# A four-layer network in one kernel: scalar work moved into the feed-forward loops, low-rank transposes between two chunks, two heads normalised on ACT

## The chip, the core and the metric

The kernel runs on one core of one Trainium2 chip. The metric is the device time of one execution, in microseconds; the number given is the median of several executions. TensorE (PE in the profile) multiplies matrices, VectorE (DVE), ScalarE (ACT) and GpSimd (POOL) work elementwise, SyncE (SP) issues the weight transfers. Each engine takes its own instructions strictly in order, and waits on semaphores for the others.

## The reference, cut to what matters

One sequence of 256 tokens with 1024 features goes through four layers in fp32. `first_block` has two: pooling and causal attention, then a gated linear recurrence (RG-LRU), each followed by a gated feed-forward network (FFN) with a three-tap causal convolution and 2816 hidden features. `second_block` has two hybrid layers:

```python
h = rms_norm_2(x, g_mix);  proj = h @ w_in          # c_q c_kv k_r d_q d_k d_v s_q s_k s_v gates
q = (rms_norm_2(c_q, g_q_lora) @ w_uq)              # low rank: 256 -> 8 heads of 96
kv = (rms_norm_2(c_kv, g_kv_lora) @ w_ukv)          # low rank: 128 -> 8 heads of 64 + 64
o_mla = softmax(rope(q) @ rope(k).T) @ v            # 8 heads
o_diff = (softmax_1 - lam * softmax_2) @ d_v        # 4 heads, position bias
o_win = window_attention(s_q, s_k, s_v, sink)       # 8 heads, position bias, band of 128
x = x + (sum of sigmoid(gate_b) * (o_b @ w_branch_b)) @ w_out
x = x + (gelu(conv(h @ w_gate)) * (h @ w_up)) @ w_down
x = x + sigmoid(rms_norm_2(x, g_ple_in) @ w_ple_gate) * rms_norm_2(pe @ w_ple_proj, g_ple)
```

The recurrence needs `softplus(-rg_lambda)`; `lam` is made of two exponentials of dot products; `rope` needs the cosine and sine of positions times 16 frequencies; the position biases need |q - k| as a 256 by 256 table.

## The kernel before, in words

All activations stay on the chip, 256 tokens as two halves (t) of 128. The weights (252 MB) are streamed once: `_push` (L247) issues the transfer of the next chunk of 128 x 2048 on SP, and ACT and DVE split it into a high part `hi` (L262) and a residual `lo` (L263), in two halves of 1024 columns each. `chunk` (L269) keeps two chunks ahead of the one in use; a buffer is free for the next chunk when TensorE has finished with the chunk three before. Each product is three matmuls (`mm3`, L277: high x high and the two mixed ones), 128 x 512 or 128 x 256 at a time. PSUM has eight banks under four tags: A (3), S (2), T (2), O (1).

The stages follow each other in `build` (L334): pooled attention, FFN, recurrence, FFN, hybrid layer 0, hybrid layer 1, each hybrid layer ending with an FFN and a gated addition of `pe`. The order of the instructions on each engine is made by a scheduler from the program order, which serves as priority, and from its own estimate of when operands are ready: an instruction may rise past earlier ones that are not ready. What goes through `vec_o`, `act_o`, `pool_o` or `sync_o` (`InOrder`, L199) is pinned behind the instruction written just before it for the same engine; in the attention of a hybrid layer TensorE too is pinned (L1272).

What the change touches:

- `norm` (L368) opens a stage: the residual sum is updated on DVE (L339), eight feature tiles are transposed (L384) and split into `xh` (ACT, L389) and `xl` (DVE, L390), and the first matmuls follow. `norm_rows` (L404) makes the row factors.
- `ffn` (L608): 22 rounds j. Each takes one chunk of two 128-wide columns blocks (48 matmuls), scales, convolves, gates (L638, L649) and splits the result; every second round from j = 5 on also multiplies a chunk of the down projection (24 matmuls of 512 columns).
- `softplus` (L656) computes two small factors for the recurrence: 2 instructions on ACT (absolute value, exponential) and, with the two halved biases of L695, 28 on DVE, all pinned. `rglru` (L688) calls it ahead of its `norm`.
- `before_b` (L795) runs between the start of the second FFN and its loop (L614): `positions` (L747) loads positions and band on POOL's queue, makes the distance tables and the cosine and sine (24 DVE instructions, 3 on ACT), then `layer_scalars(0)` (L799; 18 on DVE, 2 exponentials on ACT). `layer_scalars(1)` runs at the head of hybrid layer 1 (L1203). All are pinned.
- `hybrid` (L1199): `mla_prep` (L926) makes the low-rank vectors c, `proj` (L1021) the difference queries dq and keys dk, two chunks each; then `mla_low_rank` (L949) transposes c (6 transposes, L956) and splits it (L958, L959), and `mla_heads` (L963) multiplies by the next weights.
- `heads` (L1060) writes out the attention as bursts by hand: each burst names some steps (queries and keys `mq`, scores and softmax `ms`, transposes `mt`, values `mo` of two heads) and how many pieces of the query, gate and branch projections follow on TensorE. `normal` (L1071) multiplies the exponentials of a head by the reciprocals of their sums on POOL (L1074); `normalise` (L922) does the same on ACT.
- Behind the attention, ahead of the FFN, `pe` is loaded on POOL's queue (L1291) and split (L1293; the split's own lines are L311 and L312), not pinned.

Of the kernel before, what the change touches and what calls it, by code (L numbers as in the profile page):

```python
# [19 lines left out]
P = 128  # L20
S = 256
# [188 lines left out]
class Net:  # L210
# [69 lines left out]
        mm(out, ah, bl, start=False, stop=False)  # L280
        mm(out, al, bh, start=False, stop=stop)  # L281

    def tm_block(self, banks, n, xh, xl, nk, per):

        for k0 in range(0, nk, per):
            wh, wl = self.chunk(per, n)
            for t in range(2):
                for k in range(per):
                    kk = k0 + k
                    self.mm3(banks[t][:, :n], xh[:, kk, t * P:t * P + P], xl[:, kk, t * P:t * P + P],  # L290
                             wh[:, k, :], wl[:, k, :], kk == 0, kk == nk - 1)
# [178 lines left out]
    def pool_attn(self):  # L470
# [64 lines left out]
            self.split(ah[:, c, :], al[:, c, :], ob[:, :S])  # L535

        u = proj("AA")
        mt = self.t([P, 4, 384], "w6")
        self.sync_o.dma_start(mt, self.ap["pool"].rearrange("p (g c) -> p g c", g=4))
        pw = self.t([P, 4, P], "hg")  # L540
# [64 lines left out]
                                    in1=self.rb[:, None, :].to_broadcast([P, 2, S]), op=ALU.mult)  # L605
        return z

    def ffn(self, gi, body, ahead=None):  # L608
        xh, xl = self.norm(gi, self.acc)
        first = self.fm_first(xh, xl)  # L610
        self.norm_rows()
        acc = None
        if ahead is not None:
            ahead()  # L614
        done = []
        for j in range(NF):
            if j % 2 == 0:
                hh, hl = self.t([P, 2, S], "hg", F32R), self.t([P, 2, S], "hg", F32R)
                done.append((hh, hl))
            z = self.times_r(self.t([P, 2, S], "s"), first[j] if j < 2 else self.fm(xh, xl, "TS"[j % 2]))  # L620
            m = body(j, z[:, 0, :], z[:, 1, :])
            self.split(hh[:, j % 2, :], hl[:, j % 2, :], m)
            if j % 2 and j > 2 * LAG:
                if acc is None:
                    acc = self.wide_banks()
                kk = j - 1 - 2 * LAG
                self.tm_wide(acc, *done[kk // 2], kk, False)
        for kk in range(NF - 2 * LAG, NF, 2):
            self.tm_wide(acc, *done[kk // 2], kk, kk == NF - 2)
        self.acc = acc  # L630

    def ffn_a(self, l, gi, ahead=None):
        nc = self.nc

        def body(j, u, g):
            u = self.conv(u, f"fw{l}", f"fb{l}", j, 3, (2, 1, 0))
            g = self.conv(g, f"fw{l}", f"fb{l}", NF + j, 3, (2, 1, 0))
            nc.scalar.activation(g, g, AF.Gelu_apprx_tanh)  # L638
            nc.vector.tensor_tensor(out=g, in0=g, in1=u, op=ALU.mult)
            return g  # L640

        self.ffn(gi, body, ahead)

    def ffn_b(self, i, gi):
        nc = self.nc

        def body(j, u, g):
            g = self.conv(g, f"cw{i}", f"cb{i}", j, 3, (1, 0, -1))
            nc.scalar.activation(g, g, AF.Gelu_apprx_tanh)  # L649
            nc.vector.tensor_tensor(out=g, in0=g, in1=u, op=ALU.mult)  # L650
            return g

        self.ffn(gi, body)


    def softplus(self):  # L656

        nc = self.nc
        v = self.vec_o
        lam = self.vecs[:, self.vat["rlam"]:self.vat["rlam"] + NR]  # L660
        tl = lambda: self.t([P, 16], "ty")[:, :NR]
        e, den, s, s2, acc, out, half = (tl() for _ in range(7))
        self.act_o.activation(e, lam, AF.Abs)
        self.act_o.activation(e, e, AF.Exp, scale=-1.0)
        v.tensor_scalar(den, e, 2.0, None, op0=ALU.add)
        v.reciprocal(den, den)
        v.tensor_tensor(out=s, in0=e, in1=den, op=ALU.mult)
        v.tensor_tensor(out=s2, in0=s, in1=s, op=ALU.mult)
        v.tensor_scalar(acc, s2, 1.0 / 19, 1.0 / 17, op0=ALU.mult, op1=ALU.add)
        for n in (15, 13, 11, 9, 7, 5, 3, 1):  # L670
            v.tensor_tensor(out=acc, in0=acc, in1=s2, op=ALU.mult)
            v.tensor_scalar(acc, acc, 1.0 / n, None, op0=ALU.add)
        v.scalar_tensor_tensor(acc, acc, 2.0, s, op0=ALU.mult, op1=ALU.mult)
        v.tensor_scalar(out, lam, -1.0, 0.0, op0=ALU.mult, op1=ALU.max)
        v.tensor_tensor(out=out, in0=out, in1=acc, op=ALU.add)
        r4 = self.t([P, NR], "rg4")
        r2 = self.t([P, NR], "rg2")
        v.tensor_scalar(r4, out, -4.0, None, op0=ALU.mult)
        v.tensor_scalar(r2, out, 2.0, None, op0=ALU.mult)
        return r4, r2  # L680

    def after(self, ins, group):

# [4 lines left out]
    def rglru(self, gi):  # L688
        nc = self.nc
        act = nc.scalar.activation  # L690
        neg4, pos2 = self.softplus()
        half = self.t([P, 2 * NR], "rgh")
        for c, name in enumerate(("rba", "rbx")):
            o = self.vat[name]
            self.vec_o.tensor_scalar(half[:, c * NR:c * NR + NR], self.vecs[:, o:o + NR], 0.5, None, op0=ALU.mult)  # L695
        xh, xl = self.norm(gi, self.acc)
        wa = self.t([P, NR, P], "w6")
        wx = self.t([P, NR, P], "w6")
# [48 lines left out]
    def positions(self):  # L747
# [6 lines left out]
        band = self.t([P, 512], "bias")  # L754
        self.pool_o.dma_start(band, self.ap["band"])
        qf = self.t([P, 2], "posqf")
        v.tensor_copy(qf, pq)
        kf = self.t([P, S], "w2")
        v.tensor_copy(kf, pk)
        self.dist = self.t([P, 2, S], "dist")  # L760
        self.distw = self.t([P, 2, S], "distw")
        for t in range(2):
            v.tensor_scalar(self.dist[:, t, :], kf, qf[:, t:t + 1], None, op0=ALU.subtract)
        self.act_o.activation(self.dist[:, :, :], self.dist[:, :, :], AF.Abs)
        v.tensor_tensor(out=self.distw[:, :, :], in0=self.dist[:, :, :], in1=band.rearrange("p (t s) -> p t s", t=2), op=ALU.add)
        ang = self.t([P, 2, 16], "ang")
        for t in range(2):
            v.tensor_scalar(ang[:, t, :], self.row("freq", 16), qf[:, t:t + 1], None, op0=ALU.mult)
        self.trig = []
        two_pi = 2.0 * math.pi  # L770
        parts, rest = [], two_pi
# [7 lines left out]
        for name, quarter in (("cos", 0.25), ("sin", 0.0)):  # L779
# [3 lines left out]
            v.tensor_scalar(k, k, magic, None, op0=ALU.add)  # L783
            v.tensor_scalar(k, k, -magic, None, op0=ALU.add)
            src = ang
            for p in parts:
                v.scalar_tensor_tensor(r, k, -p, src, op0=ALU.mult, op1=ALU.add)
                src = r
            if quarter:
                v.tensor_scalar(r, r, math.pi / 2, None, op0=ALU.add)  # L790
            v.tensor_scalar(r, r, lim, -lim, op0=ALU.min, op1=ALU.max)
            self.act_o.activation(r, r, AF.Sin)
            self.trig.append(r)

    def before_b(self):  # L795
        self.positions()
        self.layer_scalars(0)

    def layer_scalars(self, i):  # L799

# [2 lines left out]
        es = []  # L803
        for a in "12":
            pr = self.t([P, 64], "lampr")
            sm = self.t([P, 16], "ty")
            v.tensor_tensor(out=pr, in0=self.row(f"lamq{a}{i}", 64), in1=self.row(f"lamk{a}{i}", 64), op=ALU.mult)
            v.tensor_reduce(sm[:, 0:1], pr, axis=AX.X, op=ALU.add)
            self.act_o.activation(sm[:, 0:1], sm[:, 0:1], AF.Exp)
            es.append(sm)  # L810
        init = 0.8 - 0.6 * math.exp(-0.3 * i)
        self.neglam = self.t([P, 1], "neglam")
        v.scalar_tensor_tensor(self.neglam, es[1][:, 0:1], -init, es[0][:, 0:1], op0=ALU.add, op1=ALU.subtract)
# [2 lines left out]
        for n in "qk":  # L816
            for nm, tb, hf in (("c1", cos, 0), ("s2", sin, 1), ("c2", cos, 1), ("s1", sin, 0)):
                r = self.t([P, 2, 16], f"rp{n}{nm}")
                g = self.row(f"mr{n}{i}", 32)[:, None, hf * 16:hf * 16 + 16].to_broadcast([P, 2, 16])
                v.tensor_tensor(out=r, in0=tb, in1=g, op=ALU.mult)  # L820
                self.rope_t[n + nm] = r
        self.gm = self.vprod(self.vec(f"mgq{i}"), self.vec(f"mgk{i}"), 96 ** -0.5)
        self.gd = self.vprod(self.vec(f"dgq{i}"), self.vec(f"dgk{i}"), 64 ** -0.5)
        self.gw = self.vprod(self.vec(f"wgq{i}"), self.vec(f"wgk{i}"), 64 ** -0.5)
# [193 lines left out]
    def slopes(self, h):  # L1018
        return 2.0 ** (-8.0 * (h + 1) / 12.0)

    def proj(self, xh, xl, heads):  # L1021
        b = [self.bank("A"), self.bank("A")]
        self.tm_block(b, 512, xh, xl, KD, 4)
        z = self.t([P, 2, 512], "w4")
        self.copy_out(b, 512, z)
        if heads:
# [33 lines left out]
    def heads(self, i, mla, diff, win):  # L1060
# [32 lines left out]

        def ms(c):
            sps = [self.scores(z[:96, :S], z[:96, S:]) for z in qk["m", c]]
            pr["m", c] = [normal(*self.softmax(sp, FULL)) for sp in sps]

        def mt(c):
            turn(("m", c), pr["m", c])
# [99 lines left out]
    def hybrid(self, i, g0):  # L1199
        nc = self.nc  # L1200
        xh, xl = self.norm(g0, self.acc, self.pending)
        if i:
            self.layer_scalars(i)  # L1203
        c, kr, skr = self.mla_prep(i, xh, xl)
        self.norm_rows()
        dq = self.proj(xh, xl, 8)
        dk = self.proj(xh, xl, 8)
        ch, cl = self.mla_low_rank(i, c)
        q4, k4, v = self.mla_heads(ch, cl, kr, skr)
        dv = self.proj(xh, xl, 0)  # L1210
        wk, wv = self.window_kv(xh, xl)
# [75 lines left out]
            self.tm_wide(acc, mh[:, kk:kk + 2, :], ml[:, kk:kk + 2, :], kk, kk == 6)  # L1287
        self.acc = acc

        pe = self.t([P, 2, S], "w2")  # L1290
        nc.gpsimd.dma_start(pe, self.ap["pe"][i])  # L1291
        peh, pel = self.t([P, 2, S], "w4", F32R), self.t([P, 2, S], "w4", F32R)
        self.split(peh[:, :, :], pel[:, :, :], pe[:, :, :])  # L1293
        self.ffn_b(i, g0 + 1)


        xh, xl = self.norm(g0 + 2, self.acc)
# [35 lines left out]

    def build(self):
        nc = self.nc
        steps = [self.start, self.pool_attn, lambda: self.ffn_a(0, 1), lambda: self.rglru(2), lambda: self.ffn_a(1, 3, self.before_b),
                 lambda: self.hybrid(0, 4), lambda: self.hybrid(1, 7)]
        update = None
        for n, f in enumerate(steps[:self.upto + 1]):
# [25 lines left out]
```

## Time and profile before

| | us |
|---|---|
| median of 3 runs | 1517.9 |
| the runs | 1517.53, 1517.9, 1520.76 |
| the profiled execution | 1523.45 |
| its span, first to last instruction | 1521.7 |
| TensorE busy | 1501.2 (99%) |
| VectorE busy | 1141.3 (75%) |
| ScalarE busy | 913.6 (60%) |
| GpSimd busy | 119.8 (8%) |

The profile is one execution. Times in rows are counted from the start of its span. The ends of matmuls are modelled, so that matmuls overlap in the rows and idle time in brackets is a lower figure; the starts are measured. "<-" after an idle time names what ended it. A line of the timeline that ends in x8 holds eight instructions that follow each other. L207 is the helper of pinned instructions, whatever calls it; then the tile names tell them apart (s: scores, T, S, A, O: banks, pT: transposed scores, qk: queries and keys, st, hi, lo: the weight chunk).

### The profile page before, as it was taken

To read this page: it belongs to the slowest core of one execution; us is meant where nothing else is said; L and a number is where in the kernel's file an instruction comes from. 1 tells how busy PE (TensorE), PEld (TensorE's weight loads), DVE (VectorE), ACT (ScalarE), POOL (GpSimd) and SP (SyncE) were. 2 spreads that over 40 slices of the span, in tenths; PEclk is the share of its full clock that TensorE was granted. 3 is DMA by queue.
4 is the path that set the end of the run, shared out by engine and by line. 5 is a ranking of instruction groups with operands and counts; after the bars stand their busy time and mean duration, and the time that the engine had idled before them with its cause. 6 is when DMAs were issued, how large, how long until landed. Compare 5 with 4: busy or idle time off the path is not lost.

```text
span 1521.7 us, 25363 instructions
## 1 busy us (share of the span) xinstructions
PE 1501.2 (99%) x10020; PEld 1356.4 (89%) x10020; DVE 1141.3 (75%) x2197; ACT 913.6 (60%) x1615; POOL 119.8 (8%) x109
## 2 busy tenths in 40 slices
PE   8999999999999999999999999999999999999998
PEld 6789999898999998889988999988889988999986
DVE  6659777789897777966867866668885877866666
ACT  6756555686775556755665545556856664654454
POOL 0200000000000000022530000000023250000000
PEclk9999999999999999999999999999999999999999
DMA  8445554445464554533334555544453344455551
GB/s 290 166 170 193 191 191 174 165 139 183 151 219 169 194 183 151 208 119 115 137 131 166 182 181 191 182 178 159 170 194 112 123 148 167 166 194 173 188 194 56
DMA packets 37879, 257.34 MB, mean 169 GB/s; under 512 B 4384, under 2 KB 4768, under 8 KB 8320
## 3 DMA queue, kind: packets, MB, share of 16 engines
q1 hardware_dynamic: 36576, 252.38, 46.8%
q0 software_dynamic: 896, 3.28, 0.6%
q8 instruction: 78, 1.28, 0.3%
q14 instruction: 41, 0.34, 0.1%
q10 hardware_dynamic: 288, 0.07, 0.0%
HBM read 254.66 MB, written 1.05 MB: 168 GB/s over the span
## 4 chain that ended last, share of the span: by engine, by line
PE 92%; DVE 3%; ACT 2%; POOL 1%; issue 1%; DMA 1%; SPq 0%; DVEq 0%
PE A L207 11%; PE A L279 11%; PE A L280 11%; PE A L281 10%; PE S L281 6%; PE S L280 6%; PE S L279 6%; PE T L281 6%; PE T L280 6%; PE T L279 6%; PE O L279 2%; PE O L280 2%; PE O L281 2%; PE S L207 2%; PE T L207 2%; PE O L207 1%
## 5 line engine op out<-in xcount | busy, mean ns | idle before, releaser
L263 DVE TENSOR_TENSOR lo<-st,hi 128x1024 fp32r<-128x1024 f32 (+3 forms) x480 | 573.6, 1209 | 129.4 <-ACT hi L262 126.7
L262 ACT ACTIVATE hi<-st 128x1024 fp32r<-128x1024 f32 (+3 forms) x480 | 489.2, 1043 | 264.4 <-PE T L280 109.7
L281 PE MATMUL S<-xh,lo 128*128 128x256 f32 x752 | 213.9, 284 | 0.0
L280 PE MATMUL S<-xl,hi 128*128 128x256 f32 x752 | 213.0, 283 | 0.0
L279 PE MATMUL S<-xh,hi 128*128 128x256 f32 x752 | 211.7, 282 | 0.0
L281 PE MATMUL T<-xh,lo 128*128 128x256 f32 x704 | 200.3, 285 | 0.0
L280 PE MATMUL T<-xl,hi 128*128 128x256 f32 x704 | 199.7, 284 | 0.0
L279 PE MATMUL T<-xh,hi 128*128 128x256 f32 x704 | 198.8, 282 | 0.0
L279 PEld LDWEIGHTS S<-xh,hi 128*128 128x128 f32 x752 | 142.5, 190 | 0.1
L281 PEld LDWEIGHTS S<-xh,lo 128*128 128x128 f32 x752 | 142.0, 189 | 0.1
L280 PEld LDWEIGHTS S<-xl,hi 128*128 128x128 f32 x752 | 141.5, 188 | 0.0
L279 PEld LDWEIGHTS T<-xh,hi 128*128 128x128 f32 x704 | 133.4, 189 | 1.6
L280 PEld LDWEIGHTS T<-xl,hi 128*128 128x128 f32 x704 | 132.5, 188 | 1.5
L281 PEld LDWEIGHTS T<-xh,lo 128*128 128x128 f32 x704 | 133.0, 189 | 0.1
L1074 POOL TENSOR_SCALAR s<-s,at 128x256 f32<-128x256 f32 x64 | 68.4, 1085 | 647.8 <-DVE ty L324 347.8
L280 PE MATMUL A<-lo,hg 128*128 128x512 f32 x294 | 116.3, 396 | 0.5 <-DVE lo L263 0.5
L279 PE MATMUL A<-hi,xh 128*128 128x512 f32 (+2 forms) x304 | 116.4, 385 | 0.2 <-ACT xh L389 0.2
L280 PE MATMUL A<-lo,xh 128*128 128x512 f32 (+2 forms) x304 | 116.3, 382 | 0.0
L279 PE MATMUL A<-hi,hg 128*128 128x512 f32 x294 | 116.2, 395 | 0.0
L281 PE MATMUL A<-hi,hg 128*128 128x512 f32 x294 | 116.2, 395 | 0.0
L281 PE MATMUL A<-hi,xl 128*128 128x512 f32 (+2 forms) x304 | 115.7, 383 | 0.0
L207 PE MATMUL A<-xh,hi 128*128 128x256 f32 x384 | 113.7, 296 | 0.0
(366 smaller groups left out, 3120.4 us busy)
## 6 DMA issues: line engine op xcount, KB each, us to landing
st<-in_w_dram SPq DMA_DIRECT2D x230, 1024.0 KB, 4.8
st<-in_w_dram SPq DMA_DIRECT2D x4, 832.0 KB, 4.5
st<-in_w_dram SPq DMA_DIRECT2D x2, 768.0 KB, 4.3
x<-in_x_dram SPq DMA_DIRECT2D x2, 512.0 KB, 5.0
st<-in_w_dram SPq DMA_DIRECT2D x4, 256.0 KB, 6.4
st<-in_w_dram SPq DMA_DIRECT2D x2, 512.0 KB, 3.5
w<-in_gain_dram POOLq DMA_DIRECT2D x2, 512.0 KB, 4.6
out_dram<-x SPq DMA_DIRECT2D x4, 256.0 KB, 2.0
```

Source lines behind the costliest of these rows:

```text
L207: return lambda *a, **k: self.tc.keep_in_program_order(f(*a, **k))
L262: nc.scalar.activation(hi[:, c0:c1], st[:, c0:c1], AF.Copy)
L263: nc.vector.tensor_tensor(out=lo[:, c0:c1], in0=st[:, c0:c1], in1=hi[:, c0:c1].bitcast(F32), op=ALU.subtract)
L279: mm(out, ah, bh, start=start, stop=False)
L280: mm(out, ah, bl, start=False, stop=False)
L281: mm(out, al, bh, start=False, stop=stop)
L1074: nc.gpsimd.tensor_scalar(s[:, c], s[:, c], r[:, t:t + 1], None, op0=ALU.mult)
```

## The change

1. `softplus`, with the halved biases, is called in `pool_attn` behind the projection u, and leaves its results in `rg_scalars`.
2. `before_b`, `positions` and `layer_scalars` become generators. `ffn` takes such a generator as `aside` and takes one piece from it at the head of each round j from 2 to 19. The second FFN gets `before_b` in 13 pieces; the two sines stand together in the last piece of `positions`.
3. The FFN of each hybrid layer gets a generator that loads `pe`, in layer 0 then makes the scalars of layer 1, and three pieces later splits `pe`. The load is now pinned on POOL.
4. `proj` for dk takes `middle`, called between its two chunks, and there `mla_low_rank` runs.
5. Of the eight heads of the first attention, the two of c = 0 are normalised by `normalise` on ACT.

```diff
-    def tm_block(self, banks, n, xh, xl, nk, per):
+    def tm_block(self, banks, n, xh, xl, nk, per, middle=None):
         for k0 in range(0, nk, per):
+            if k0 and middle is not None:
+                middle()
             wh, wl = self.chunk(per, n)
...
         u = proj("AA")
+        self.softplus()
...
     def ffn(self, gi, body, aside=None):
...
-        if ahead is not None:
-            ahead()
         for j in range(NF):
+            if aside is not None and 2 <= j < NF - 2:
+                next(aside, None)
...
     def positions(self):
...
+        kf = self.t([P, S], "w2")
+        yield
         v.tensor_copy(qf, pq)
-        kf = self.t([P, S], "w2")
         v.tensor_copy(kf, pk)
...
+        yield
         self.act_o.activation(self.dist[:, :, :], self.dist[:, :, :], AF.Abs)
         v.tensor_tensor(out=self.distw[:, :, :], in0=self.dist[:, :, :], ...)
+        yield
...
+        for r in self.trig:
             self.act_o.activation(r, r, AF.Sin)
-            self.trig.append(r)
+        yield
...
     def layer_scalars(self, i):
...
             self.act_o.activation(sm[:, 0:1], sm[:, 0:1], AF.Exp)
             es.append(sm)
+        yield
...
                 self.rope_t[n + nm] = r
+            yield
...
         def ms(c):
             sps = [self.scores(z[:96, :S], z[:96, S:]) for z in qk["m", c]]
-            pr["m", c] = [normal(*self.softmax(sp, FULL)) for sp in sps]
+            pr["m", c] = []
+            for sp in sps:
+                s, r = self.softmax(sp, FULL)
+                if c == 0:
+                    self.normalise(s, FULL, r)
+                else:
+                    normal(s, r)
+                pr["m", c].append(s)
...
         xh, xl = self.norm(g0, self.acc, self.pending)
-        if i:
-            self.layer_scalars(i)
...
         dq = self.proj(xh, xl, 8)
-        dk = self.proj(xh, xl, 8)
-        ch, cl = self.mla_low_rank(i, c)
+        low = []
+        dk = self.proj(xh, xl, 8, lambda: low.extend(self.mla_low_rank(i, c)))
+        ch, cl = low
...
-        pe = self.t([P, 2, S], "w2")
-        nc.gpsimd.dma_start(pe, self.ap["pe"][i])
-        peh, pel = self.t([P, 2, S], "w4", F32R), self.t([P, 2, S], "w4", F32R)
-        self.split(peh[:, :, :], pel[:, :, :], pe[:, :, :])
-        self.ffn_b(i, g0 + 1)
+        halves = []
+        def aside():
+            pe = self.t([P, 2, S], "w2")
+            self.pool_o.dma_start(pe, self.ap["pe"][i])
+            yield
+            if i == 0:
+                yield from self.layer_scalars(1)
+            for _ in range(3):
+                yield
+            halves.extend([self.t([P, 2, S], "w4", F32R), self.t([P, 2, S], "w4", F32R)])
+            self.split(*(z[:, :, :] for z in halves), pe[:, :, :])
+        self.ffn_b(i, g0 + 1, aside())
+        peh, pel = halves
```

## Rows read from the trace of the kernel before

**Rows 1.** The page: busy time, share of the span and instructions of each engine.
```profile
PE 1501.2 (99%) x10020; PEld 1356.4 (89%) x10020; DVE 1141.3 (75%) x2197; ACT 913.6 (60%) x1615; POOL 119.8 (8%) x109
```

**Rows 2.** Timeline of PE (start, us, engine, line, operation): matmuls of the second FFN.
```profile
425.46 0.39 PE L281 MATMUL A<-hi,hg 128*128 128x512 f32 x1
425.69 0.40 PE L279 MATMUL A<-hi,hg 128*128 128x512 f32 x1
426.59 0.50 PE L280 MATMUL A<-lo,hg 128*128 128x512 f32 x1 [0.50 <-DVE lo L263]
```

**Rows 3.** Timeline of PE: low-rank transposes of layer 0 and what follows them.
```profile
613.88 0.38 PE L956 MATMUL T<-ident,w 128*128 128x128 f32 x2
614.10 0.38 PE L956 MATMUL S<-ident,w 128*128 128x128 f32 x2
614.97 0.44 PE L279 MATMUL A<-hi,o 128*128 128x384 f32 x1 [0.49 <-ACT o L958]
```

**Rows 4.** Timeline of PE: start of the recurrent stage, then of the second FFN.
```profile
289.36 0.60 PE L384 MATMUL S<-ident,x 128*128 128x128 f32 x4
...
295.81 0.28 PE L279 MATMUL S<-xh,hi 128*128 128x256 f32 x1
...
387.89 0.60 PE L384 MATMUL S<-ident,x 128*128 128x128 f32 x4
...
393.05 0.28 PE L279 MATMUL S<-xh,hi 128*128 128x256 f32 x1
```

**Rows 5.** Timeline of PE: first and last attention rows of layer 0, then layer 1.
```profile
650.10 0.60 PE L207 MATMUL T<-ident,w 128*96 128x128 f32 x4
...
793.59 1.08 PE L207 MATMUL O<-pT,wv 128*64 128x256 f32 x8
...
1122.44 0.60 PE L207 MATMUL T<-ident,w 128*96 128x128 f32 x4
...
1257.98 1.08 PE L207 MATMUL O<-pT,wv 128*64 128x256 f32 x8
```

**Rows 6.** Windows: us, busy (x) PE, PEld, DVE, ACT, POOL, granted clock, DMA share, GB/s.
```profile
662.00:672.00 10.00, 7.59 (x30) 6.22 (x30) 2.76 (x5) 3.24 (x10) 4.73 (x5) 0.66 0.28 105
763.00:771.00 8.00, 5.63 (x33) 4.54 (x32) 5.76 (x16) 6.98 (x18) 2.95 (x2) 0.79 0.09 17
1134.00:1144.00 10.00, 8.86 (x67) 7.70 (x66) 5.42 (x10) 5.97 (x17) 6.46 (x5) 1.00 0.29 107
```

**Rows 7.** Timeline of layer 0: POOL's first normalising, and PE's first transpose of its result.
```profile
659.66 6.02 POOL L1074 TENSOR_SCALAR s<-s,at 128x256 f32<-128x256 f32 x4 [251.43 <-DVE at L919]
662.18 0.27 PE L207 MATMUL T<-ident,s 128*128 128x128 f32 x1
```

**Rows 8.** Timeline of PE: the same transposes in layer 1.
```profile
1134.52 0.71 PE L207 MATMUL T<-ident,s 128*128 128x128 f32 x5
1136.37 0.55 PE L207 MATMUL T<-ident,s 128*128 128x128 f32 x3 [1.14 <-POOL s L1074]
```

**Rows 9.** Timeline of layer 1: the split of pe on ACT, and PE after it.
```profile
1229.43 0.63 ACT L311 ACTIVATE w<-w 128x512 fp32r<-128x512 f32 x1 [6.08 <-DMA w<-in_pe_dram]
1232.55 0.44 PE L207 MATMUL O<-pT,wv 128*64 128x256 f32 x2 [0.57 <-ACT pT L853]
```

**Rows 10.** Lines: softplus's commonest DVE instruction, stretch 285 to 300.
```profile
L207 DVE TENSOR_SCALAR ty<-ty 128x10 f32<-128x10 f32 x10 | 1.7, 168 | 0.1
```

**Rows 11.** Windows: end of pooled attention, rest of the second FFN, third FFN.
```profile
70.00:97.00 27.00, 26.89 (x123) 21.12 (x122) 14.11 (x16) 13.21 (x21) 2.12 (x4) 1.00 0.55 195
430.00:580.00 150.00, 150.00 (x1020) 138.64 (x1019) 116.46 (x179) 83.81 (x129) 0.00 (x0) 1.00 0.55 192
840.00:1050.00 210.00, 210.00 (x1401) 192.35 (x1399) 149.21 (x229) 114.04 (x170) 0.00 (x0) 1.00 0.52 184
```

**Rows 12.** Lines: ACT's table loads in the stretch 405 to 422.
```profile
L207 ACT ACT_TABLE_LOAD x3 | 3.8, 1283 | 0.1
```

**Rows 13.** Lines by form: ACT's normalising in pooled attention.
```profile
L924 ACT ACTIVATE s<-s,at 128x256 f32<-128x256 f32 x8 | 4.0, 496 | 0.0
```

More of the change, by code (lines that the diff above doesn't have):

```diff
@@ L606, in times_r, with ffn @@
         return z
-    def ffn(self, gi, body, ahead=None):
+    def ffn(self, gi, body, aside=None):
         xh, xl = self.norm(gi, self.acc)
@@ L630, in ffn, with ffn_a @@
         self.acc = acc
-    def ffn_a(self, l, gi, ahead=None):
+    def ffn_a(self, l, gi, aside=None):
         nc = self.nc
@@ L640, in body, with ffn_b @@
             return g
-        self.ffn(gi, body, ahead)
-    def ffn_b(self, i, gi):
+        self.ffn(gi, body, aside)
+    def ffn_b(self, i, gi, aside):
         nc = self.nc
@@ L651, in body @@
             return g
-        self.ffn(gi, body)
+        self.ffn(gi, body, aside)
     def softplus(self):
@@ L679, in softplus @@
         v.tensor_scalar(r2, out, 2.0, None, op0=ALU.mult)
-        return r4, r2
+        half = self.t([P, 2 * NR], "rgh")
+        for c, name in enumerate(("rba", "rbx")):
+            o = self.vat[name]
+            v.tensor_scalar(half[:, c * NR:c * NR + NR], self.vecs[:, o:o + NR], 0.5, None, op0=ALU.mult)
+        self.rg_scalars = r4, r2, half
     def after(self, ins, group):
@@ L690, in rglru @@
         act = nc.scalar.activation
[L691 to L695, printed above, removed]
+        neg4, pos2, half = self.rg_scalars
         xh, xl = self.norm(gi, self.acc)
@@ L791, in positions @@
             v.tensor_scalar(r, r, lim, -lim, op0=ALU.min, op1=ALU.max)
+            self.trig.append(r)
+            yield
+        for r in self.trig:
             self.act_o.activation(r, r, AF.Sin)
-            self.trig.append(r)
+        yield
     def before_b(self):
-        self.positions()
-        self.layer_scalars(0)
+        yield from self.positions()
+        yield from self.layer_scalars(0)
     def layer_scalars(self, i):
@@ L805, in layer_scalars @@
             pr = self.t([P, 64], "lampr")
-            sm = self.t([P, 16], "ty")
+            sm = self.t([P, 1], "sm" + a)
             v.tensor_tensor(out=pr, in0=self.row(f"lamq{a}{i}", 64), in1=self.row(f"lamk{a}{i}", 64), op=ALU.mult)
@@ L821, in layer_scalars @@
                 self.rope_t[n + nm] = r
+            yield
         self.gm = self.vprod(self.vec(f"mgq{i}"), self.vec(f"mgk{i}"), 96 ** -0.5)
@@ L1019, in slopes, with proj @@
         return 2.0 ** (-8.0 * (h + 1) / 12.0)
-    def proj(self, xh, xl, heads):
+    def proj(self, xh, xl, heads, middle=None):
         b = [self.bank("A"), self.bank("A")]
-        self.tm_block(b, 512, xh, xl, KD, 4)
+        self.tm_block(b, 512, xh, xl, KD, 4, middle)
         z = self.t([P, 2, 512], "w4")
@@ L1288, in hybrid @@
         self.acc = acc
-        pe = self.t([P, 2, S], "w2")
-        nc.gpsimd.dma_start(pe, self.ap["pe"][i])
-        peh, pel = self.t([P, 2, S], "w4", F32R), self.t([P, 2, S], "w4", F32R)
-        self.split(peh[:, :, :], pel[:, :, :], pe[:, :, :])
-        self.ffn_b(i, g0 + 1)
+        halves = []
+        def aside():
+            pe = self.t([P, 2, S], "w2")
+            self.pool_o.dma_start(pe, self.ap["pe"][i])
+            yield
+            if i == 0:
+                yield from self.layer_scalars(1)
+            for _ in range(3):
+                yield
+            halves.extend([self.t([P, 2, S], "w4", F32R), self.t([P, 2, S], "w4", F32R)])
+            self.split(*(z[:, :, :] for z in halves), pe[:, :, :])
+        self.ffn_b(i, g0 + 1, aside())
+        peh, pel = halves
         xh, xl = self.norm(g0 + 2, self.acc)
@@ L1335, in build @@
         nc = self.nc
-        steps = [self.start, self.pool_attn, lambda: self.ffn_a(0, 1), lambda: self.rglru(2), lambda: self.ffn_a(1, 3, self.before_b),
+        steps = [self.start, self.pool_attn, lambda: self.ffn_a(0, 1), lambda: self.rglru(2), lambda: self.ffn_a(1, 3, self.before_b()),
                  lambda: self.hybrid(0, 4), lambda: self.hybrid(1, 7)]
```

## The prediction

> **What bounds the kernel now.** First the page: TensorE is busy for 99% of the span, the other engines far less [rows 1]. Matmul ends are modelled there, so busy time cannot show a lost microsecond; I read the starts in TensorE's timeline. In a full stretch one 512-column matmul starts 0.23 us after the last (425.46 to 425.69) [rows 2], and two 128-column transposes take 0.22 (613.88 to 614.10) [rows 3]. Whatever exceeds these steps is lost. From one end of the trace to the other the losses beyond half a microsecond are few, apart from the ramp at the very start, which the diff leaves alone:
> - After the position tables, 425.69 to 426.59: 0.90 for a 0.23 step, 0.67 lost, waiting for a weight residual on DVE [rows 2].
> - After the low-rank transposes, 614.10 to 614.97: two transposes are 0.22, 0.65 lost, waiting for ACT [rows 3].
> - At the start of the recurrent stage. From the first norm transposes to the first S matmul it takes 6.45 us (289.36 to 295.81); the second FFN's start runs the same transposes and matmuls in 5.16 (387.89 to 393.05). 1.29 more [rows 4].
> - In the attention of the hybrid layers. The stretch is the same code twice: 143.49 us in layer 0, 135.54 in layer 1, 7.95 apart [rows 5]. The windows say what 5.1 of that is: layer 0's granted clock is 0.66 over 10 us and 0.79 over 8 us, a mixture of the 2.4 and 1.2 GHz levels (10 x 0.34 + 8 x 0.21 = 5.1), each after TensorE had waited, while layer 1 has 1.00 [rows 6]. The first wait: POOL normalises two heads from 659.66 to 665.68 and TensorE is ready to transpose them at 662.18 [rows 7]. Layer 1 waits there too, 1134.52 to 1136.37 less five transposes (0.55): 1.30 [rows 8]. The second: ACT stands 6.08 us in front of a split whose input, pe, is still in flight; behind it in ACT's queue are copies that TensorE needs, and TensorE idles 0.57 in layer 1 [rows 9].
>
> So TensorE bounds, and only waits of its own, with the low clock behind two of them, can be won.
>
> **The change part by part.** The sum is made on the profiled execution, 1523.45 us (span 1521.7 and 1.75 around it). It is 5.55 over the median of the runs, 1517.9; I return to that.
>
> *Softplus into pooled attention.* 28 DVE and 2 ACT instructions leave the norm. At 0.17 us each the DVE part is 4.7 [rows 10]. Its new place, after the copy of u, has DVE busy 14.11 of 27 us and ACT 13.21 [rows 11]; that idle time hides it. Exp's table is loaded there already by the softmax. If the cover were gone, the pooled residuals would be late by part of the 4.7; I take 0 to 0.4. The load that preceded softplus moves to the first tanh; it is 1.28 us [rows 12], in a stage that feeds TensorE from other chunks meanwhile. Gain 1.29: the norm becomes like its sister.
>
> *Position tables and layer 0's scalars into the second FFN's loop*, 13 pieces from j = 2 on. 42 DVE and 5 ACT instructions stay in this stage but no longer in one bunch; the two Sin share one table load, one load fewer. The three POOL transfers queue behind finished work. The later loop has DVE 78% and ACT 56% busy [rows 11], which covers a piece of one to two microseconds in each round. Gain 0.67; late next would be a residual again, 0 to 0.67.
>
> *Layer 1's scalars into the third FFN.* 18 small DVE and 2 Exp. DVE there is 71%, ACT 54% busy [rows 11]. The Exp needs its own table, then gelu's again: two loads, 2 x 1.28 = 2.6 us of ACT [rows 12] beside 96 us of idle ACT time, taken as 0. The Trainium skill (ScalarE: Activation LUTs, "What ACT_TABLE_LOAD costs" and "Rules for kernel authors") wants functions grouped by table set and counts a drain with each switch, 2.66 us in all; by that the two switches would take 5.3 us of ACT. The rows show 1.28 for the load and no drain as an item of its own.
>
> *Low-rank transposes between the chunks of dk.* Six transposes, three ACT and three DVE instructions in each layer, earlier by one chunk: 24 steps of 0.23, 5.6 us. Their input is ready by then, since all of dq lies between. The 0.65 goes in each layer: 1.30 [rows 3]. The heads then start right behind dk in a third bank; the copy of dk's first bank is issued before dk ends, so I add nothing.
>
> *Two heads per layer on ACT instead of POOL.* Four ACT instructions of 0.50 [rows 13] against 6.02 us on POOL [rows 7]: from 659.66 they end at 661.7, before the transposes at 662.18. The new wait: ACT's queue now stands until the reciprocal, and behind it are the copies of the next queries and keys (their T banks the transposes need) and weight casts two chunks ahead. The margin is 0.5 us in layer 0, over 2 in layer 1. Bounds of what remains: 0 and layer 1's present 1.30 per layer; I take 0.5 in all, nearer 0 as POOL's time shrinks to a third.
>
> *pe's transfer and split into the third and fourth FFN.* The transfer is pinned behind POOL's last normalising; the split may still rise in ACT's queue, but with the attention nearly over. Bounds per layer 0 and 0.57; I take 0.3 in all.
>
> Sum: attention gains layer 1's 1.30 + 0.57 = 1.87, and layer 0 the same plus its 7.95: 11.69. With 1.29 + 0.67 + 1.30 that is 14.95. Against it 0.5 + 0.3 and 0.2 for the pieces in the loops (bounds 0 and 4): net 14.0. The profiled execution would come to 1509.5.
>
> **The median.** The runs span 1517.53 to 1520.76, 3.2 apart, about one of the two low-clock episodes (3.4 and 1.7), and the profiled one lies 5.55 above the median where both together are 5.1. I therefore take the median run as having neither: 14.0 - 5.1 = 8.9 to gain, 1517.9 - 8.9 = 1509.0. Both ways lead to the same number, because the changed kernel should have no episode. The Trainium skill (TensorE: Matmul & The Clock Gate, "What's actually happening") says that the number of slow matmuls varies from run to run of one kernel; by it the timed runs need not share the profile's 5.1, and the sum would be the 1509.0. If they do share it, all 14.0 come off: 1503.9.
>
> **The rivals.**
> - *The timed runs do have the low clock*: 1503.9. For: 5.55 could be what profiling costs. Against: the runs' own spread of 3.2. Chance 0.12.
> - *The wait moves from POOL to ACT*: the normalising is issued behind casts, and TensorE waits as now at full clock. Costs 1.30 twice and at most the 2.85 (7.95 - 5.1) by which layer 0's waits are longer: up to 5.45, 1514.5. For: a margin of 0.5. Chance 0.10.
> - *pe's split rises and blocks ACT again*, so that the change does not do what it says: 0.57 twice and the 2.85, 1513.0. For: its order is not pinned. Against: few copies are left behind it. Chance 0.08. Both of these together: 3.74 + 2.85 = 6.6, 1515.6, chance 0.05.
> - *The table loads show*: 2.6 us, 1511.6. The Trainium skill's rule on table sets, named above, points this way. Against: a cover of 96 us. Chance 0.03.
> - *Slower: the pieces stall the FFN loops.* Each of 21 pieces (13 and 8) pins DVE and ACT instructions that wait for each other behind the weight casts. If each cost TensorE what the bunch cost once, 0.67, that is 14.1: 1523.1. It turns slower from 0.57 a piece. Against: the FFN rows at 78% and 71%, and that the whole bunch cost 0.67. Chance 0.07.
>
> **How the numbers follow.** The forecast has 0.55, by itself 1506 to 1512. About 0.2% (3.0 us, 1514.9 to 1520.9) is what a measurement of this kernel can tell from no change. Faster: 0.55 + 0.12 + 0.08 + 0.03 and half of the POOL rival, which ends at the limit: 0.83. Same: its other half and the double case: 0.10. Slower: 0.07. The range 1502.5 to 1516.5 takes in all but the slower case and the ends of two others.
>
> **What would show it.** Right: the recurrent stage's start near 5.2 us; no step of 0.9 after the position tables; low-rank transposes inside dk and nothing lost behind them; granted clock 1.00 all through both layers' attention, their two stretches within 1 us of each other near 134; ACT never standing for pe. Wrong: ACT idle before the normalising, with TensorE waiting for ACT at the first transposes of scores; a new step over 0.5 us in an FFN loop; low clock in a new place; or attention clean in the trace and the median above 1515, which would say that the timed runs never lost what the profile shows.

## The result, and the profile after

The changed kernel takes 1504.33 us (four runs, 1503.80 to 1504.67) against 1519.33 for the kernel before on the same chip (1517.53 to 1520.76): ratio 0.9902, 95% interval 0.9884 to 0.9919. That is faster, 4.7 us lower than the 1509.0 forecast, and inside the range. The profiled execution fell by 19.4 us (1523.45 to 1504.07, span 1502.3) where 14.0 was forecast.

The page after, to be held against [rows 1]:

```profile
PE 1489.8 (99%) x10020; PEld 1352.5 (90%) x10020; DVE 1140.8 (76%) x2197; ACT 919.6 (61%) x1626; POOL 108.1 (7%) x101
```

TensorE's share is 99% in both, so it tells nothing of the 19.4; the starts do.

**Attention** (against [rows 5, 6, 7]). The timeline of the changed kernel, first and last attention rows of layer 0, then of layer 1; then ACT's normalising and TensorE's transposes of its result in layer 0; then two windows of layer 0 (columns as in [rows 6]):

```profile
645.04 1.03 PE L207 MATMUL T<-ident,w 128*96 128x128 f32 x8
...
778.43 1.08 PE L207 MATMUL O<-pT,wv 128*64 128x256 f32 x8
...
1105.79 1.04 PE L207 MATMUL T<-ident,w 128*96 128x128 f32 x8
...
1239.06 1.08 PE L207 MATMUL O<-pT,wv 128*64 128x256 f32 x8
```

```profile
655.62 1.71 ACT L937 ACTIVATE s<-s,at 128x256 f32<-128x256 f32 x4 [0.43 <-DVE at L932]
...
657.12 1.03 PE L207 MATMUL T<-ident,s 128*128 128x128 f32 x8
```

```profile
657.00:667.00 10.00, 10.00 (x79) 9.07 (x78) 6.70 (x11) 8.88 (x20) 3.85 (x4) 1.00 0.31 107
...
760.00:770.00 10.00, 10.00 (x85) 9.30 (x84) 6.61 (x16) 7.43 (x19) 6.82 (x7) 1.00 0.31 107
```

The two layers now take 133.39 and 133.27 us (143.49 and 135.54 before). Eight transposes stand in one row without a wait, ACT stood only 0.43 us for the reciprocal, and the granted clock is 1.00 where it was 0.66 and 0.79.

**The recurrence** (against [rows 4]): the start of its stage, then of the second FFN, then its output projection.

```profile
287.45 0.60 PE L386 MATMUL S<-ident,x 128*128 128x128 f32 x4
...
292.63 0.28 PE L279 MATMUL S<-xh,hi 128*128 128x256 f32 x1
...
373.87 0.40 PE L280 MATMUL A<-lo,hg 128*128 128x512 f32 x1
374.90 0.50 PE L281 MATMUL A<-hi,hg 128*128 128x512 f32 x1 [0.63 <-DVE hg L314]
...
385.55 0.60 PE L386 MATMUL S<-ident,x 128*128 128x128 f32 x4
...
390.78 0.28 PE L279 MATMUL S<-xh,hi 128*128 128x256 f32 x1
```

Its start takes 5.18 us, like its sister's 5.23 (6.45 before). But there is a step that the kernel before did not have: 1.03 us at 373.87, 0.80 of it lost, for a residual on DVE.

**A gain where nothing was edited.** The first FFN lies between two norms, 98.68 to 289.36 before (190.68 us) and 97.82 to 287.45 after (189.63): 1.05 us less, with the same instructions. The first line of each timeline below is its start, and its end is the start of the recurrence, 289.36 [rows 4] and 287.45. Of the two operands in a row the first is the moving one and the second the stationary one. One pass of the stage shows why it is shorter: 24 matmuls of 512 columns with hg as the stationary side, the wide ones (from the second to the third start below), then 96 of 256 columns, the narrow ones (third to fourth start). Timeline of PE, before and after:

```profile
98.68 0.60 PE L384 MATMUL S<-ident,x 128*128 128x128 f32 x4
...
152.71 0.40 PE L279 MATMUL A<-hi,hg 128*128 128x512 f32 x1
...
158.31 0.28 PE L279 MATMUL T<-xh,hi 128*128 128x256 f32 x1
...
169.83 0.40 PE L279 MATMUL A<-hi,hg 128*128 128x512 f32 x1
```

```profile
97.82 0.60 PE L386 MATMUL S<-ident,x 128*128 128x128 f32 x4
...
151.77 0.39 PE L279 MATMUL A<-hi,hg 128*128 128x512 f32 x1
...
157.27 0.28 PE L279 MATMUL T<-xh,hi 128*128 128x256 f32 x1
...
168.79 0.40 PE L279 MATMUL A<-hi,hg 128*128 128x512 f32 x1
```

The 24 take 5.60 us before and 5.50 after, 233.3 and 229.2 ns a step; the 96 take 11.52 in both, 120.0 ns. Over all such steps of the trace the means are 233.4 and 229.4 ns. There are four FFNs with 264 and the recurrence with 120: 1176 x 4.0 ns = 4.7 us, at full granted clock and with no wait. The ramp at the start came out 0.9 shorter (98.68 to 97.82), which is no gain of the change: with the same instructions it ended at 98.73 in another trace (the second run of experiment 1). 14.0 + 4.7 + 0.9 = 19.6 is near the profile's 19.4, but the 14.0 is the forecast and not a measurement; how it was made up in fact stands in the part on the prediction.

What changed for hg is its address. The softplus tiles (64 + 64 + 96 bytes a partition) are now first used in pooled attention, so the allocator places them ahead of the tags w6 and hg, which move up by 224 bytes: hg from 201120 to 201344, while the weight buffers hi stay at 52672. The distance from hi, the moving side, to hg, modulo 128 bytes, goes from 96 to 64.

### The profile page after: what moved, and what is told of

Read it like the earlier page. It is cut to its first block, busy times and chain, and to the rows that moved or that the text cites. A ratio compares the mean times of both kernels' runs of the same rounds, so it can differ in the third digit from the quotient of the medians.

```text
span 1502.3 us, 25361 instructions
## 1 busy us (share of the span) xinstructions
PE 1489.8 (99%) x10020; PEld 1352.5 (90%) x10020; DVE 1140.8 (76%) x2197; ACT 919.6 (61%) x1626; POOL 108.1 (7%) x101
## 3 DMA queue, kind: packets, MB, share of 16 engines
HBM read 254.66 MB, written 1.05 MB: 170 GB/s over the span
## 4 chain that ended last, share of the span: by engine, by line
PE 95%; DVE 3%; issue 1%; ACT 1%; DMA 0%; SPq 0%; ACTq 0%
PE A L207 14%; PE A L279 10%; PE A L280 10%; PE A L281 10%; PE S L281 6%; PE S L280 6%; PE S L279 6%; PE T L281 6%; PE T L280 6%; PE T L279 6%; PE T L207 2%; PE S L207 2%; PE O L280 2%; PE O L279 2%; PE O L281 2%; PE O L207 2%
## 5 line engine op out<-in xcount | busy, mean ns | idle before, releaser
L207 PE MATMUL A<-xh,lo 128*128 128x256 f32 x384 | 108.2, 282 | 0.0
```

What stands on the lines that cost most here:

```text
L207: return lambda *a, **k: self.tc.keep_in_program_order(f(*a, **k))
```

## The experiments

All times are medians; ratios are to the kernel before on the same chip (1517.84 us in the first group of four, 1520.24 in the second, 1517.90 in the third). Each group had a chip of its own. The lowest time of the kernel before on the three is 1516.29, 1516.88 and 1516.57, so a difference of half a microsecond between groups, or from the changed kernel's 1504.33, shows nothing.

**1. The place alone, from both sides.** A pad in the kernel before, and 32 bytes in the changed one:

```diff
+        self.t([P, 56], "pad")
         mt = self.t([P, 4, 384], "w6")
```

> The kernel before, with nothing but an unused pad of 224 bytes a partition ahead of the tag w6, so that hg lies 224 bytes higher, where the changed kernel has it. Theory P (place): some 4.7 us of the change's gain come from this shift; the 512-column matmuls with hg as the stationary side step from 233.4 to about 229.4 ns, all four FFNs get about 1.0 us shorter, and the time falls by 4.7 us, ratio 0.997. Rival E (the timed runs lost the low clock too): the shift does nothing, steps stay at 233.4 ns, ratio 1.000; the shorter steps of the changed kernel are then due to something else.

```diff
-        half = self.t([P, 2 * NR], "rgh")
+        half = self.t([P, 2 * NR + 8], "rgh")
```

> The changed kernel, with the tile rgh 32 bytes wider, so that w6 and hg lie 32 bytes higher and no instruction differs. P: the address is again 32 above a multiple of 128 as in the kernel before, the steps with hg go back to 233.4 ns and the time rises by 4.7 us, from 1504.3 to 1509.0. E: no change, 1504.3.

Measured: 1513.93, ratio 0.9975 (0.9964 to 0.9986), 3.9 us less than before; and 1509.25, ratio 0.9941 (0.9929 to 0.9953), 4.9 more than the changed kernel's 1504.33. The mean steps with hg are 229.4 and 233.4 ns in these two. The changed kernel with 32 bytes more, same pass:

```profile
153.02 0.40 PE L279 MATMUL A<-hi,hg 128*128 128x512 f32 x1
...
158.62 0.28 PE L279 MATMUL T<-xh,hi 128*128 128x256 f32 x1
```

5.60 us again. So the place gives 4 to 5 us, and the edits by themselves, with hg at its old distance, give 1517.84 - 1509.25 = 8.6.

**2. Which place?** First every large tag at a multiple of 128:

```diff
-        self.ident = self.t([P, P], "ident")
+        self.ident = self.t([P, P + 16], "ident")[:, :P]
...
-        ss = self.t([P, 2, 2], "ssx")
+        ss = self.t([P, 2, 16], "ssx")[:, :, :2]
...
-        self.r = self.t([P, 2], "r")
+        self.r = self.t([P, 24], "r")[:, :2]
...
-        half = self.t([P, 2 * NR], "rgh")
+        half = self.t([P, 2 * NR + 12], "rgh")
```

> The changed kernel with small tiles widened so that every large tag (x, st, hi, lo, xh, xl, w2, bias, w4, o, qk, s, pT, w6, hg) begins at a multiple of 128 bytes; no instruction differs. P, if it is the stationary side's address that counts: the 512-column steps with xh and o stationary fall from 232.4 and 233.4 to about 229.4 ns, some 570 steps of 3 to 4 ns, 2 us, 1502.3; if it holds for the 256-column steps with hi and lo stationary too (7000 of 118 to 121 ns, to 115 to 117 ns), up to 15 to 20 us more. E: no change, 1504.3.

Measured: 1503.45 (ratio 0.9903, 0.9890 to 0.9915), about the changed kernel's time. All 512-column steps became 232.3, those with hg too, which rose: a multiple of 128 is not it. The narrow passes fell from 11.52 to 11.39 us, which hides that loss in the time. Sorted by distance from hi, every row so far fitted, and the next kernel put the two sides 64 apart by widening one more tile, then the mirror image by taking ident's padding away:

```diff
-        self.ones = self.t([P, P], "ones")
+        self.ones = self.t([P, P + 16], "ones")[:, :P]
```

> The changed kernel with hi and lo at multiples of 128 bytes and xh, xl, o and hg 64 above one; no instruction differs. Rows so far, by the distance of the stationary tile from the moving one modulo 128: 96 gives 233.4 ns a 512-column step (hg before, o), 0 gives 232.3 to 232.4 (xh everywhere, hg in the aligned kernel), 64 gives 229.4 (hg as changed). If that distance decides (D64): all 512-column steps go to 229.4, those with xh and o too, 570 steps of 3 to 4 ns, 2 us; the 256-column steps, whose two sides are then 64 apart as well, fall by as much a column or more, 1.5 ns or more of 118.7 on 7000, 10 us: 1492. If the absolute place decides (hg at a multiple of 128): hg's steps are 232 to 233, 1504 to 1509.

```diff
-        self.ident = self.t([P, P + 16], "ident")[:, :P]
+        self.ident = self.t([P, P], "ident")
```

> The changed kernel with hi and lo left 64 above a multiple of 128 and xh, xl, o and hg moved to a multiple: the distance between the two sides is 64 as in place64, the absolute places are exchanged. D64: 256-column steps of 114 to 116 ns and 1474 again. If the absolute place of hi and lo (a multiple of 128) made place64 fast: steps of 118 to 120 ns, 1503. What speaks against a rule by distance alone is the run with the staggered hg, whose steps did not fall into its classes.

Measured: 1473.98 (ratio 0.9700, 0.9683 to 0.9716) and 1473.66 (0.9706, 0.9693 to 0.9719), both 30 us under the changed kernel. The same pass in the first and in its mirror:

```profile
150.48 0.39 PE L279 MATMUL A<-hi,hg 128*128 128x512 f32 x1
...
155.97 0.28 PE L279 MATMUL T<-xh,hi 128*128 128x256 f32 x1
...
166.88 0.39 PE L279 MATMUL A<-hi,hg 128*128 128x512 f32 x1
```

```profile
150.28 0.39 PE L279 MATMUL A<-hi,hg 128*128 128x512 f32 x1
...
155.78 0.28 PE L279 MATMUL T<-xh,hi 128*128 128x256 f32 x1
...
166.69 0.39 PE L279 MATMUL A<-hi,hg 128*128 128x512 f32 x1
```

The 96 narrow matmuls went from 11.52 to 10.91 us, 113.6 ns each. Exchanging the absolute places changes nothing, so between hi at 0 and xh, o and hg at 64, or the reverse, it is the distance that counts. These two kernels moved the other tiles behind them along; only hg was moved nearly by itself (experiment 1), so for the narrow matmuls it is argued, not shown, that the distance of their own two operands does it. I expected 1492: the narrow steps fell by 5 to 6 ns and not by 1.5.

**3. A finer map** of the distance, hg's buffers 2080 bytes apart:

```diff
+        if tag == "hg":
+            n = int(np.prod(shape[1:]))
+            z = pool.tile([P, 520], dt, tag=tag, ...)[:, :n]
+            return z if len(shape) == 2 else z.rearrange("p (a b) -> p a b", a=shape[1])
```

> The changed kernel with hg's eight buffers 2080 bytes apart and not 2048, so that they lie 0, 32, 64 and 96 further on modulo 128, in turn (distance from hi: 64, 96, 0, 32, and again); no instruction differs. D64: the steps of the 512-column matmuls fall into classes by buffer: 229.4 at 64, 233.4 at 96, 232.3 at 0, and a value not seen yet at 32; the time rises by about the mean excess, 3 ns on 1175, 2 to 4 us, 1507. If the place is not the cause: all stay at 229.4, 1504.3.

Measured: 1503.66 (0.9896, 0.9876 to 0.9916). Sorted by the distances of a matmul and of the next one, the steps do not fall into the expected classes: means from 228.6 to 232.3 ns, and 238.2 for one order of two distances (0, then 32), with no fixed value for one distance. The FFNs' mean wide step rose to 231.8, and 24 of the 32 narrow passes, whose operands had not moved, took 11.39 us and not 11.52, which cancels it. So distance is the rule for a whole kernel laid out at 64, and not a price for each matmul by itself. Open.

**4. The parts, undone one at a time** in the changed kernel, the buffers unmoved. First the two heads on POOL again:

```diff
-                if c == 0:
-                    self.normalise(s, FULL, r)
-                else:
-                    normal(s, r)
+                normal(s, r)
```

> The changed kernel with the two heads of c = 0 normalised on POOL again, all else as changed. If the wait at the first transposes of scores is a plain wait as in layer 1 (1.30 us in each layer): 2.6 us slower, 1506.9. If layer 0's wait is as long as in the profile of before and the low clock follows in the timed runs (E): 1.30 + 1.30 + up to 2.3 + 3.4 us, as much as 8.4 us slower, 1512.7, with a granted clock under 0.7 over 10 us behind the wait. If the wait was hidden otherwise: 1504.3.

Measured: 1515.36 (0.9973, 0.9962 to 0.9984), 11.0 slower. Its timeline in layer 0, and two windows:

```profile
657.96 0.27 PE L207 MATMUL T<-ident,s 128*128 128x128 f32 x1
659.51 0.55 PE L207 MATMUL T<-ident,s 128*128 128x128 f32 x3 [1.28 <-POOL s L1087]
660.92 0.47 PE L207 MATMUL T<-ident,s 128*128 128x128 f32 x1 [0.87 <-POOL s L1087]
661.82 0.47 PE L207 MATMUL T<-ident,s 128*128 128x128 f32 x1 [0.42 <-POOL s L1087]
```

```profile
656.65 5.12 POOL L1087 TENSOR_SCALAR s<-s,at 128x256 f32<-128x256 f32 x4 [230.97 <-DVE at L932]
```

```profile
660.00:670.00 10.00, 8.71 (x41) 7.64 (x41) 1.92 (x6) 3.58 (x11) 4.73 (x6) 0.66 0.29 105
1125.00:1135.00 10.00, 7.57 (x40) 6.47 (x41) 2.98 (x6) 3.53 (x11) 5.09 (x6) 0.83 0.32 107
```

Three steps lose 1.55 + 1.14 + 0.90 less three transposes, 3.26 us, in layer 0, and 3.18 in layer 1. TensorE is ready 1.31 us behind POOL's start, where it was 2.52 before [rows 7]. The windows add 3.4 + 1.7 of low clock. Of the twelve runs, eight have a mean granted clock of 0.995 or 0.996 and take 1514.99 to 1516.51; four have 0.998 or 0.999 and take 1510.27 to 1512.02. The sum says the same: 1504.3 + 6.4 = 1510.7, and 5.1 more is 1515.8.

The same part alone in the kernel before (the lines above, added there):

> The kernel before with the two heads of c = 0 normalised on ACT and nothing else changed; hg stays where it was. If the attention's first wait is what a timed run shows: layer 1's 1.30 and layer 0's 2.94 (three steps of 1.75, 0.62 and 0.90 less 0.33), 4.2 us, 1513.6, and no clock under 0.999 behind it in layer 0's first scores. If layer 1's 1.30 twice is all: 1515.2. If the undone normalising of the changed kernel (11.0 us) is its price here too: 1506.8.

Measured: 1512.77 (0.9969, 0.9959 to 0.9979), 5.1 less, near the 4.2. The rest lies at the second wait, which shrank as well (step of 2.08 to 0.53). So this part is worth 5 us where the others are missing and 11 where they are there. The 11 are not waits alone: in the changed kernel TensorE comes to POOL's work sooner, 6.4 of waits where it was 4.2, and the rest is the low clock, which eight of twelve runs had there, against two of twelve of the kernel before in this group (0.997 and 0.998).

Then pe ahead of the FFN, the low-rank transposes behind dk, and softplus and tables:

```diff
+        pe = self.t([P, 2, S], "w2")
+        nc.gpsimd.dma_start(pe, self.ap["pe"][i])
+        halves.extend([self.t([P, 2, S], "w4", F32R), self.t([P, 2, S], "w4", F32R)])
+        self.split(*(z[:, :, :] for z in halves), pe[:, :, :])
...
         self.ffn_b(i, g0 + 1, aside())
```

> The changed kernel with pe's transfer and split back behind the attention, ahead of each FFN and not pinned; all else as changed. If the split rises and ACT stands in front of it, as before: 0.57 to 2.4 us in each layer (layer 1's and layer 0's rows), 1.1 to 4.8 us in all, 1505.4 to 1509.1, and low clock behind it where the wait is long. If POOL's shorter work lets the transfer start earlier, so that pe has arrived: 1504.3.

```diff
-        low = []
-        dk = self.proj(xh, xl, 8, lambda: low.extend(self.mla_low_rank(i, c)))
-        ch, cl = low
+        dk = self.proj(xh, xl, 8)
+        ch, cl = self.mla_low_rank(i, c)
```

> The changed kernel with the low-rank transposes behind dk again. By the sum: 0.65 in each layer comes back, 1.3 us, 1505.6. Rival (they are hidden elsewhere by now): 1504.3.

```diff
-        self.softplus()
+        for z, n in (("rg4", NR), ("rg2", NR), ("rgh", 2 * NR)):
+            self.t([P, n], z)
...
+        self.softplus()
         neg4, pos2, half = self.rg_scalars
...
+        if gi == 3:
+            for _ in aside:
+                pass
         done = []
```

> The changed kernel with softplus and the halved biases back in the recurrence, ahead of its norm, and the position tables and layer 0's scalars back in one bunch ahead of the second FFN's loop; the small tiles still get their place early, so that no buffer moves. By the terms of the sum: 1.29 at the recurrence's start and 0.67 in the second FFN come back, 1.96 us, 1506.3. Rival (the pieces in the loop cost what they saved): 1504.3 or less.

Measured: pe 1506.04 (0.9913, 0.9895 to 0.9930), 1.7 slower; low rank 1505.39 (0.9916, 0.9902 to 0.9930), 1.1 slower; softplus and tables 1504.79 (0.9904, 0.9886 to 0.9921), 0.5 slower, which is within the scatter between chips. ACT in front of pe again and TensorE behind it (layer 1); the low-rank wait; the tables' wait:

```profile
1212.56 0.63 ACT L313 ACTIVATE w<-w 128x512 fp32r<-128x512 f32 x1 [6.35 <-DMA w<-in_pe_dram]
...
1215.68 1.08 PE L207 MATMUL O<-pT,wv 128*64 128x256 f32 x8 [0.57 <-ACT pT L866]
```

```profile
610.83 0.44 PE L279 MATMUL A<-hi,o 128*128 128x384 f32 x1 [0.49 <-ACT o L971]
```

```profile
425.86 0.50 PE L280 MATMUL A<-lo,hg 128*128 128x512 f32 x1 [0.50 <-DVE lo L263]
```

Each old wait comes back with its old size. In the last kernel the recurrence's start is 6.45 again, but the step at 374 is gone, and the stage takes 98.00 us against 98.10.

**5. The kernel before at the good place**, with the four widened tiles and nothing of the change:

> The kernel before with the buffers' places of place64, and nothing of the change. Place and the change's parts independent: 1517.8 less the 30.4 of place64 (1504.3 to 1474.0) and less the 4.9 that hg's shift gave the change, 1482.6; the changed kernel at the same places, 1474.0, is then 8.6 faster, the sum that the prediction made for the parts being 8.9. If faster stages turn waits that were hidden into open ones, the difference is larger than 8.6.

Measured: 1489.31 (0.9809, 0.9796 to 0.9823): the change is worth 15.3 at this place, not 8.6. The faster matmuls reach POOL's work earlier, and all four of its runs have a mean granted clock of 0.997 or 0.998, so part of the 15.3 is low clock (3.4 in the window below). Timeline in layer 0 and 1, and the window behind:

```profile
652.29 0.55 PE L207 MATMUL T<-ident,s 128*128 128x128 f32 x3 [2.02 <-POOL s L1074]
...
1109.15 0.33 PE L207 MATMUL T<-ident,s 128*128 128x128 f32 x1 [1.74 <-POOL s L1074]
```

```profile
1109.00:1119.00 10.00, 9.27 (x46) 8.19 (x48) 2.31 (x5) 3.65 (x11) 4.63 (x6) 0.66 0.30 107
```

Of the 16.3 between the two profiled executions the hybrid layers make 5.0 and 7.1 and the second FFN 4.9 (the start gives 0.5 back). Of the 4.9, 1.8 are the tables' two waits (steps of 1.35 and 0.89), and 3.1 are a slower rhythm of the narrow matmuls behind them (last section).

## Why the prediction was right, and where it was not

- **What bounds the kernel**: right. Every wait named was there, went when its part was changed and came back when it was undone.
- **"The median": right.** The step took the median run to hold no episode of low clock. Beside these kernels the one before ran 37 times: 25 runs have a mean granted clock of 0.999 or 1.000 and a median of 1517.45, 12 have 0.997 or 0.998 and 1520.2. The profiled one, 0.997 and 1523.45, was one of the rarer runs with both. What they cost it can be read off the kernel before with the pad, whose trace has the same three steps behind POOL's work and a clock of 1.000: layer 0's attention takes 138.90 us there and not 143.49, so 4.6, near the 5.1 made from the windows. What the Trainium skill says (TensorE: Matmul & The Clock Gate, "What's actually happening"), that slow matmuls vary from run to run of one kernel, agrees: 1516.29 to 1522.07 here, at clocks of 1.000 to 0.997. The 8.9 forecast on that basis is the 8.6 measured with hg at its old distance, and the 1509.0 is the 1509.25 of that kernel. That the two agree so well is in part luck. Held against that same trace (attention 138.90 and 135.66, span 10.0 longer, 0.7 of it the ramp at the start), the attention gave 5.5 + 2.4 = 7.9 us where the sum, without low clock, has 11.69 - 5.1 - 0.8 = 5.8; the rest gave 1.4 where it has 3.1.
- **The step that failed: the sum had no term for where the buffers lie**, and so put it at nothing. "Net 14.0", and 8.9 for the median, counts instructions and waits; the softplus edit was costed as "28 DVE and 2 ACT instructions leave the norm". It also moved 224 bytes of tiles ahead of hg, worth 4.9 us, more than any edit but the normalising. The first rival, timed runs with the low clock, gave 1503.9 and looks like the outcome, but its mechanism isn't: the changed kernel with hg 32 bytes higher keeps every edit and takes 1509.25.
- **Rule and measurement.** The runs show the pace of matmuls at full clock going with where their two operands lie to each other: 233.4 or 229.4, 120.0 or 113.6 ns. The Trainium skill (TensorE: Matmul & The Clock Gate, "Step-by-step: what each phase is for") says that the two operands are read through ports of their own and that loading the next weights takes no read bandwidth from the running matmul. If that were all, the place of one operand to the other would not matter, and the 64-byte layout would take 1504.3; it took 1474.0. No run shows which accesses meet.
- **Softplus, 1.29: right at its place, given back later.** What would be late next was put at 0 to 0.4 in pooled attention; it was a residual in the recurrence's own output projection, 0.80 at 373.87. The tables' 0.67 came as 1.02 (by so much the second FFN is longer with them undone). Of the 1.96 for both, 0.5 was measured, too little to tell from the scatter.
- **Low-rank, 1.30**: 1.1 measured. **pe, 0.57 a layer and more in layer 0, less 0.3**: 1.7. In layer 0 the split rose only to 828.98, behind the whole attention (778.43), so nothing of the 0.3 was due.
- **The normalising**: the new wait on ACT was 0.43 us and cost nothing, so the 0.5 set aside for it wasn't due. Its size alone, 5.1, agrees with the rows (1.30 and 2.94, and part of the second wait).
- **Pieces in the FFN loops**, 0.2 and the slower rival: no step over half a microsecond in any FFN. The third FFN has five table loads where it had one, since each of the two exponentials fell between two gelus; the prediction counted two more and not four. They show nowhere on TensorE.

## What to carry to other kernels

Compare a stage that nobody edited before crediting an edit: a first FFN 1.05 us shorter with the same instructions was the sign that something other than the waits had moved. Print the addresses of the operands that TensorE reads in its inner loops, before and after, and try them 64 bytes apart modulo 128: here that was worth 30 us, 2% of the kernel, for four widened tiles. And price a removed wait in the kernel that it will stand in: the same part was worth 5.1 alone and 11.0 last, nearly half of the latter through the low clock behind the wait.

## What was not expected of the hardware

- Two operands at distance 0 or 96 modulo 128 give 232.3 and 233.4 ns for 512 columns and 118.6 to 120.0 for 256; at 64, about 229 and 113.6, and in one stage 117.8 (next point). The fast pace at 64 holds for the two exchanged layouts; a distance of 32 was only tried mixed with others, without a clear value.
- One kernel can have two rhythms at a granted clock of 1.00. In the kernel before at the good place, the 96 narrow matmuls of a pass take 10.91 us in the first FFN and 11.31 in every pass of the second after the tables' wait (113.6 and 117.8 ns), with the same buffers; the changed kernel at that place takes 10.91 in both. Why it stays in the slower one to the end of the stage is open. One pass of the second FFN, from the first of these starts to the second:

```profile
439.41 0.28 PE L279 MATMUL T<-xh,hi 128*128 128x256 f32 x1
...
450.72 0.40 PE L279 MATMUL A<-hi,hg 128*128 128x512 f32 x1
```

- A low clock follows a wait in some executions of one kernel and not in others: [rows 6] had it, the twelve runs of experiment 4 had it eight times, and the profile of the kernel before with the pad has the same three steps, 1.75, 0.62 and 0.90, and a mean clock of 1.000.
